# A gated conv-MLP on one core: weights in 2 KB rows, sums of weights by transfers within SBUF, and another order of the products

## The chip, the core and the metric

The kernel is written in the Tile language for Trainium2 and runs on one core. A core has a matrix engine (TensorE, PE in the profile; its weight loads are listed apart as PEld), a vector engine (VectorE, DVE), a scalar engine (ScalarE, ACT), GpSimd (POOL) and SyncE (SP); the last two issue most of the transfers, which 16 DMA engines carry out. SBUF is the memory that the engines read, PSUM the one that PE writes its sums to, in banks. The metric is the device time of one execution in microseconds, the median of several runs.

## What is computed

The program is one inference step of a decoder layer for a prompt of 512 tokens and 8 samples of one token: a mixer, a cross-attention and, as the last third, a gated MLP with a causal convolution between its up-projection and its gate. Only the MLP is touched:

```python
def conv_ffn(xn, prefix, w_up, conv_w, conv_b, w_down):
    T = xn.shape[1]
    up = xn @ w_up
    ext = jnp.concatenate([prefix, up], axis=1)
    c = conv_b
    for k in range(CONV_W):
        c = c + conv_w[k] * ext[:, k:k + T]
    gate, val = jnp.split(c, 2, axis=-1)
    return (jax.nn.silu(gate) * val) @ w_down, ext[:, -(CONV_W - 1):]
```

`w_up` is 1024 x 5632, `w_down` 2816 x 1024, all in fp32. The 520 tokens are held as two halves of 260.

## The kernel before

Every fp32 matrix is split into a high and a low part (`split`: ACT writes `w_hi`, L117, then DVE writes `w_lo`, L120), and a product is three matmuls of 128x128 by 128x260: high by high, high by low, low by high. PE does nothing else in this stage.

*Tiles.* The up-projection is cut into 22 up tiles j of 128 gate and 128 value columns. Tiles 0 to 4 (`up_tile`) and 5, 6 (`up_classic`) are plain products. Tiles 7 to 21 (`up_seven`) take seven products instead of eight by a scheme like Strassen's. With the name of the matrix of mixed inputs of each, the steps of a tile are: s1 (B11), s5 (N1), s2 (B21), s6 (N2), s3 (B22), s7 (T3) and s4 (T4), 12 matmuls each (L1888). They write three banks: a and c are the two halves of one PSUM tile `ps_pp`, b is `ps_t`. s1, s6, s7 and s4 write a; s5 and s3 write c; s2 writes b. Behind s5 ACT copies a and c to `ext`; behind s2 DVE adds b; behind s6 ACT copies a (ext<-ps_pp 128x260); behind s3 DVE adds c (`out12`); behind s7 DVE takes a (`out22`, L1911); behind s4 ACT copies a. The dependence is kept for the PSUM tile, so a product that writes c also comes behind the eviction of a that was written ahead of it.

*Weights.* A product's weights come in units of 256 KB, 128 partitions by 512 values. There are 13 raw units (`w_u`, `raw_x`), used in turn, and a ring of four split ones. s1, s2 and s4 load one block of `w_up` with SP (L1784). s5 and s7 need the sum of two blocks: SP loads the first, then POOL loads the second on top of it with an adding transfer (`both`, L1878). s6's weights are s1's plus s5's raw unit (`sum2`), s3's are s2's plus that (`sum4`); both are adds on DVE ahead of the split (L120, w_u<-w_u and its likes, 128x512). Rows of `w_up` and `w_down` are read from memory in pieces of 128 values, 512 bytes.

*Down-projection.* It is summed over three groups of tiles, 0-6, 7-14, 15-21. The first two groups' 16 column blocks (`down`, two steps each, plain products by `classic`, L1827) stand between the tiles' steps, the rest behind them.

*What sets the order.* The list `steps` is written by hand. A loop goes through it: step m's matmuls are issued together with the split of step m+3 (AHEAD) and with the loads of up to 13 steps ahead (EARLY), as far as raw units are free. A unit is free when the split that reads it is issued; the transfer into it waits for that split and for all that read or write it before. Tile's scheduler may then still move instructions of an engine against each other.

Of the kernel before, what the change touches and what calls it, by code (L numbers as in the profile page):

```python
# [13 lines left out]
OP = mybir.AluOpType  # L14
AX = mybir.AxisListType

P = 128
D = 1024
KT = D // P
# [88 lines left out]
def decoder_step(ctx: ExitStack, tc: tile.TileContext, A, O):  # L108
# [98 lines left out]
    def blocks(hi, lo):  # L207
        return lambda k: (hi[:, k], lo[:, k])
# [1409 lines left out]

    ctx.push(open_psum("ps5", "left", pp=3, t=2))

    w_up = A["w_up"][0]
    w_down = A["w_down"][0]
    PARTS = ((0, 7), (7, 15), (15, FT))
    NA = PARTS[1][0]
    hid = {}
    hid_mid = []
    xs3 = blocks(x3_hi, x3_lo)
    acc4 = ptile(late[0], [P, 2, HT], "acc")
    last_v = last.rearrange("p b (v f) -> p v b f", v=2)

# [8 lines left out]
        ring_at[0] += n  # L1639
        return tuple(t[:, at_ % 2 * 4:at_ % 2 * 4 + 4 * n] for t in ring_w[at_ // 2 % 2])  # L1640

    def up_cols(v, j):
        return slice(v * DFF + j * P, v * DFF + (j + 1) * P)

    def up_products(j):

        raws = [raw_w[j % 2][:, 2 * v:2 * v + 2].rearrange("p u (k c) -> p (u k) c", c=P) for v in range(2)]
        for v in range(2):
            sp.dma_start(raws[v], w_up[:, up_cols(v, j)].rearrange("(k p) c -> p k c", p=P))
        for v in range(2):  # L1650
            w = ring_units(2)
            split(w[0], w[1], raws[v])
            ps = bank("pp")
            project(ps, w, xs3)
            yield ps
# [69 lines left out]
    run(chain(conv(0, 0), conv(0, 1), gate(0)))  # L1725


    NI = KT // 2
    xm4 = [ptile(actp, [P, 4, NI, HT], "act_a", F32R, bufs=2, name="xm4") for _ in range(2)]
    xm3 = ptile(ff, [P, 2, 3, NI, HT], "xm3", F32R)  # L1730
    B11, B21, B22, T3_, N1, N2, T4_ = range(7)
# [36 lines left out]
    taken = set()  # L1768
    behind = []

    def rows(src, k0, n):
        return src[k0 * P:(k0 + n) * P].rearrange("(k p) c -> p k c", p=P)

    def next_unit():
        i = unit_at[0]
        return i % NS if i < 2 * NS else (i - NS) % NU
# [1 line left out]
    def load_unit(src, n=4):  # L1778

        at_ = next_unit()  # L1780
        taken.add(at_)
        unit_at[0] += 1
        u = units[at_].rearrange("p (k c) -> p k c", c=P)[:, :n]
        sp.dma_start(u, src)  # L1784
        return at_, u

    class Step:

        def __init__(self, mm, load=None, prep=None, post=None, held=False):
            self.load_, self.prep_, self.mm_, self.post_, self.held = load, prep, mm, post, held  # L1790

        def load(self):
            if self.load_:
# [8 lines left out]
        def prep(self):  # L1802
            raw = self.prep_() if self.prep_ else self.raw
            if self.load_ and not self.held:
                self.free()
            n = raw.shape[1]
            self.w = tuple(t[:, :n] for t in ring_units(1))
            split(self.w[0], self.w[1], raw)

        def mm(self):  # L1810
            self.mm_(self.w)
# [3 lines left out]
    def classic(ps_of, src, xs, kt, post):  # L1815

        out = []
        for k0 in range(0, kt, 4):
            n = min(4, kt - k0)

            def mm(w, k0=k0, n=n):
                ps = ps_of(k0 == 0)
                for k in range(n):
                    xhi, xlo = xs(k0 + k)
                    for j, (a, x) in enumerate(((w[0], xhi), (w[0], xlo), (w[1], xhi))):
                        for hf in range(2):
                            pe.matmul(ps[:, hf, :HT], a[:, k, :], x[:, hf, :], start=(k0 + k + j == 0),  # L1827
                                      stop=(k0 + k == kt - 1 and j == 2))

            out.append(Step(mm, load=lambda k0=k0, n=n: load_unit(rows(src, k0, n), n), post=post if k0 + n == kt else None))  # L1830
        return out

    def held(tag):
# [9 lines left out]
    def up_classic(j):  # L1843
        out = []
        for v in range(2):
            ps = held("pp")

            def post(v=v, ps=ps):
                evict(j, v, ps())
                behind.append(conv(j, v))  # L1850
                if v:
                    behind.append(gate(j))

            out.append(classic(ps, w_up[:, up_cols(v, j)], xs3, KT, post))
        return out[0] + out[1]

    def down(pi, d, then=None):
        j0, j1 = PARTS[pi]
        ps = held("pp")

        def post():
            tt(hT[:, d], hT[:, d], ps()[:, :, :HT], OP.add)
            if then:
                then()

        return classic(ps, w_down[j0 * P:j1 * P, d * P:(d + 1) * P], lambda k: hid[j0 + k], j1 - j0, post)

    def up_seven(j):

        ac, bb = held("pp"), held("t")  # L1870

        def block(m, s):
            return w_up[:, up_cols(m, j)].rearrange("(i s p) c -> p s i c", s=2, p=P)[:, s]

        def both(a, b):
            def load():
                u = load_unit(a)
                pool.dma_start(u[1], b, accum_op=OP.add)  # L1878
                return u
            return load  # L1880

        def product(ps_of, x, first):
            def mm(w):
                ps = ps_of(first)
                for i in range(NI):
                    xhi, xlo = xm(x, i)
                    for q, (a, b) in enumerate(((w[0], xhi), (w[0], xlo), (w[1], xhi))):
                        pe.matmul(ps, a[:, i, :], b, start=(first and i + q == 0), stop=(i == NI - 1 and q == 2),  # L1888
                                  skip_group_check=True)
            return mm  # L1890

        a_of = lambda new: ac(new)[:, 0, :HT]
        c_of = lambda new: ac()[:, 1, :HT]
        b_of = lambda new: bb(new)[:, :HT]

        def keep():
            e = ext_tile(j)
            acopy(e.rearrange("p v r t -> p (v r) t")[:, 0:4:3, 2:], ac()[:, :, :HT])

        def out11():  # L1900
            o = exts[j][:, 0, 0, 2:]
            tt(o, o, b_of(False), OP.add)

        def out12():
            o = exts[j][:, 0, 1, 2:]
            tt(o, o, c_of(False), OP.add)
            behind.append(conv(j, 0))

        def out22():
            o = exts[j][:, 1, 1, 2:]  # L1910
            dve.scalar_tensor_tensor(o, a_of(False), -1.0, o, op0=OP.mult, op1=OP.subtract)  # L1911

        def out21():
            acopy(exts[j][:, 1, 0, 2:], a_of(False), scale=-1.0)
            behind.extend((conv(j, 1), gate(j)))

        s = {}
        s[1] = Step(product(a_of, B11, True), lambda: load_unit(block(0, 0)), held=True)
        s[5] = Step(product(c_of, N1, True), both(block(1, 0), block(1, 1)), post=keep, held=True)
        s[2] = Step(product(b_of, B21, True), lambda: load_unit(block(0, 1)), post=out11, held=True)  # L1920

        def sum2():
            tt(s[1].raw, s[1].raw, s[5].raw, OP.add)
            s[5].free()
            return s[1].raw

        def sum4():
            tt(s[2].raw, s[2].raw, s[1].raw, OP.add)
            s[1].free()
            s[2].free()  # L1930
            return s[2].raw

        s[6] = Step(product(a_of, N2, False), prep=sum2, post=lambda: acopy(exts[j][:, 0, 1, 2:], a_of(False)))
        s[3] = Step(product(c_of, B22, False), prep=sum4, post=out12)
        s[7] = Step(product(a_of, T3_, False), both(block(0, 0), block(1, 0)), post=out22)
        s[4] = Step(product(a_of, T4_, False), lambda: load_unit(block(1, 1)), post=out21)
        return s
# [1 line left out]
    steps = up_classic(NA - 2) + up_classic(NA - 1)  # L1939
    sevens = [up_seven(j) for j in range(NA, FT)]  # L1940
    downs = [down(0, d) for d in range(KT)] + [down(1, d) for d in range(KT)]
    steps += [sevens[0][i] for i in (1, 5, 2, 6, 3)]
    for n, s in enumerate(sevens):
        t = sevens[n + 1] if n + 1 < len(sevens) else None
        if n:
            steps += downs.pop(0)
        if not t:
            steps += [s[7]] + downs.pop(0) + [s[4]]
        elif n:
            steps += [s[7], t[1], t[5], s[4], t[2], t[6], t[3]]  # L1950
        else:
            steps += [t[1], t[5], s[7], t[2], s[4], t[6], t[3]]
    for x in downs:
        steps += x

# [24 lines left out]
    kt = j1 - j0  # L1980

    def tail_unit(d, k0, n):
        return load_unit(rows(w_down[j0 * P:j1 * P, d * P:(d + 1) * P], k0, n), n)

    AHEAD, EARLY, POPS = 3, 13, 2
    tail_raw = [Step(None, load=lambda d=d, k0=k0: tail_unit(d, k0, min(4, kt - k0))) for d in range(D0, KT) for k0 in (0, 4)]
# [111 lines left out]
def lay_out(x):  # L2098

    def cols(a):  # L2100
# [3 lines left out]
    xs = x["x_sample"][:, 0].reshape(2, 4, KT, P).transpose(3, 2, 0, 1)  # L2104
    pe = x["pe_cmp"][0].reshape(32, P).T
    given = {name: x[name] for name in ("cache_win", "state_pool", "state_ffn", "cache_mem",
                                        "w_pool", "w_out", "w_xq", "w_xkv", "w_xo", "w_up", "w_down")}
    given["x_t"] = np.concatenate([xp, xs], axis=3)
    given["x_row"] = x["x_prompt"][0].reshape(NQB, P, D)
    given["x_row_s"] = x["x_sample"][:, 0]  # L2110
# [3 lines left out]
    given["w_gate_t"] = x["w_in"][0][:, 1792:].reshape(KT, P, 24).transpose(1, 0, 2)  # L2114
    given["w_cmp_t"] = x["w_cmp"][0].reshape(2, 2, 8, P, 64).transpose(3, 0, 2, 1, 4)
    given["w_cmp_e"] = x["w_cmp"][0, 0].reshape(2, 8, P, 64).transpose(3, 1, 0, 2)
    pt = x["page_table"].astype(np.int32)
    given["pages"] = np.concatenate([np.broadcast_to(pt.reshape(1, 64), (P, 64)), np.repeat(pt.reshape(4, 16), 8, axis=1).T], axis=1)
    ck = x["cache_kv"][0].reshape(NPHYS, 8, 16, 4, P)
# [52 lines left out]
```

## Time and profile before

| | us |
|---|---|
| median of 3 runs | 826.23 (826.06 to 830.38) |
| the profiled execution | 827.16 |
| its span, first to last instruction | 825.5 |
| granted clock of PE, mean | 0.996 |
| PE busy, of the span | 808.1 |
| DVE, ACT, POOL busy | 605.5, 448.0, 95.3 |

The page of the profile has, for each engine, its busy time and a line of 40 digits, each the busy tenths of one slice of 20.6 us. The MLP's products fill the last third of the span, from about 448 us. The up tiles with seven products lie between about 530 and 765 us. A row of the timeline has the start, the duration, the engine, the line, the operation with out<-in and, in brackets, the idle time before it with what ended it; "x2" is two instructions in one row. Matmuls are pipelined: one starts every 0.12 us though each is listed with 0.28.

### The profile page before, as it was taken

How to read it: one execution, taken by the hardware profiler on the slowest of the kernel's cores; microseconds unless marked ns; L12 is line 12 of the kernel's file. 1: busy time of each engine (PE TensorE's matmuls, PEld its weight loads, DVE VectorE, ACT ScalarE, POOL GpSimd, SP SyncE). 2: the span in 40 equal slices, each digit the busy share in tenths (PEclk: the TensorE clock that was granted, in tenths of full speed). 3: DMA queues.
4: the chain of work that ended last, by engine and by line, in shares of the span. 5: the costliest groups of instructions: out<-in, count | busy, mean ns of one | idle time of the engine just before them, and what ended most of it. 6: DMA issues, size and time to landing. Idle time of an engine off the chain costs nothing.

```text
span 825.5 us, 17787 instructions
## 1 busy us (share of the span) xinstructions
PE 808.1 (98%) x6889; PEld 754.8 (91%) x6889; DVE 605.5 (73%) x1460; ACT 448.0 (54%) x940; POOL 95.3 (12%) x100
## 2 busy tenths in 40 slices
PE   8999999999999999999999999999999999999996
PEld 8988887987778899999799999999999999999995
DVE  5644586987657766888674799998887887887714
ACT  6742245767665553444343465666666666665541
POOL 1300210000000031000032000111111111100021
PEclk9999999999999999999999999999999999999998
DMA  9988984833222283677443224756766866754422
GB/s 327 251 270 289 413 323 155 290 123 116 77 77 53 60 256 103 204 251 255 137 115 102 75 81 123 156 135 151 166 141 147 169 145 141 158 137 120 160 123 104
DMA packets 146365, 137.87 MB, mean 167 GB/s; under 512 B 6416, under 2 KB 133264, under 8 KB 144088
## 3 DMA queue, kind: packets, MB, share of 16 engines
q1 hardware_dynamic: 127224, 114.63, 44.5%
q0 software_dynamic: 18624, 21.26, 12.3%
q8 instruction: 54, 0.88, 0.4%
q10 hardware_dynamic: 432, 0.84, 0.3%
q14 instruction: 31, 0.25, 0.1%
HBM read 129.56 MB, written 10.69 MB: 170 GB/s over the span
## 4 chain that ended last, share of the span: by engine, by line
PE 85%; DMA 6%; DVE 5%; ACT 2%; issue 1%; SPq 0%; DVEq 0%; POOL 0%; ACTq 0%
PE ps_pp L205 25%; PE ps_pp L1888 16%; PE ps_pp L1827 16%; PE ps_t L1888 3%; PE ps_o L1154 2%; PE ps_pp L2068 2%; PE ps_tb L1071 2%; PE ps_tb L1264 2%; PE ps_sc L1107 2%; DMA WT<-in_w_cmp_e_dram 2%; PE ps_tf L1139 2%; PE ps_x L1465 1%; PE ps_tb L1233 1%; DMA wc_raw<-in_w_cmp_t_dram 1%; PE ps_x L1486 1%
## 5 line engine op out<-in xcount | busy, mean ns | idle before, releaser
L1888 PE MATMUL ps_pp<-xm,w_hi 128*128 128x260 f32 x720 | 133.4, 285 | 0.1
L1888 PEld LDWEIGHTS ps_pp<-xm,w_hi 128*128 128x128 f32 x720 | 110.9, 188 | 2.3 <-ACT ext L117 0.3
L117 ACT ACTIVATE w_hi<-w_u 128x512 fp32r<-128x512 f32 (+2 forms) x110 | 72.7, 662 | 66.5 <-PE ps_pp L1888 22.7
L1888 PE MATMUL ps_pp<-xm,w_lo 128*128 128x260 f32 x360 | 101.5, 282 | 0.0
L120 DVE TENSOR_TENSOR w_lo<-w_u,w_hi 128x512 fp32r<-128x512 f32 (+2 forms) x110 | 80.1, 729 | 16.6 <-ACT w_hi L117 15.3
L1888 PEld LDWEIGHTS ps_pp<-xm,w_lo 128*128 128x128 f32 x360 | 67.7, 188 | 0.0
L120 DVE TENSOR_TENSOR hT<-hT,ps_pp 128x520 f32<-128x520 f32 (+1 forms) x44 | 28.3, 644 | 45.0 <-PE ps_pp L205 17.9
L205 PE MATMUL ps_pp<-x_hi,w_hi 128*128 128x260 f32 x288 | 60.0, 286 | 0.0
L205 PE MATMUL ps_pp<-x_hi,w_lo 128*128 128x260 f32 x288 | 59.6, 285 | 0.0
L205 PE MATMUL ps_pp<-x_lo,w_hi 128*128 128x260 f32 x288 | 58.4, 284 | 0.0
L117 ACT ACTIVATE w_hi<-w_raw 128x1024 fp32r<-128x1024 f32 (+1 forms) x38 | 35.0, 922 | 41.9 <-PE ps_pp L205 31.6
L205 PE MATMUL ps_pp<-xn_hi,w_hi 128*128 128x260 f32 x208 | 45.5, 296 | 1.9 <-ACT w_hi L117 1.9
L205 PEld LDWEIGHTS ps_pp<-x_hi,w_lo 128*128 128x128 f32 x288 | 44.9, 188 | 0.6 <-issue 0.4
L205 PEld LDWEIGHTS ps_pp<-x_hi,w_hi 128*128 128x128 f32 x288 | 44.9, 188 | 0.3
L120 DVE TENSOR_TENSOR w_lo<-w_raw,w_hi 128x1024 fp32r<-128x1024 f32 (+1 forms) x38 | 41.4, 1089 | 5.1 <-ACT w_hi L117 4.8
L1878 POOL DMA_DIRECT2D w_u<-in_w_up_dram x19 | 24.4, 1286 | 178.4 <-DMA w_u<-in_w_up_dram 106.2
L1117 ACT ACTIVATE prob<-prob,mx 128x384 f32<-128x384 f32 (+3 forms) x64 | 35.4, 555 | 17.7 <-DVE mx L1115 17.4
L205 PEld LDWEIGHTS ps_pp<-x_lo,w_hi 128*128 128x128 f32 x288 | 44.5, 188 | 0.4 <-issue 0.4
L205 PE MATMUL ps_pp<-xn_lo,w_hi 128*128 128x260 f32 x208 | 43.6, 289 | 0.1
L205 PE MATMUL ps_pp<-xn_hi,w_lo 128*128 128x260 f32 x208 | 43.5, 289 | 0.0
L120 DVE TENSOR_TENSOR w_lo<-raw_x,w_hi 128x512 fp32r<-128x512 f32 (+1 forms) x53 | 35.8, 675 | 10.3 <-ACT w_hi L117 9.7
L117 ACT ACTIVATE w_hi<-raw_x 128x512 fp32r<-128x512 f32 (+1 forms) x53 | 32.8, 618 | 18.2 <-PE ps_pp L1888 13.2
(495 smaller groups left out, 2309.1 us busy)
## 6 DMA issues: line engine op xcount, KB each, us to landing
w_u<-in_w_up_dram SPq DMA_DIRECT2D x57, 256.0 KB, 3.2
xkr<-in_cache_mem_dram SPq DMA_DIRECT2D x16, 512.0 KB, 4.7
xvr<-in_cache_mem_dram SPq DMA_DIRECT2D x16, 512.0 KB, 7.3
raw_x<-in_w_up_dram SPq DMA_DIRECT2D x26, 256.0 KB, 3.7
Kt<-in_k_t_dram SPq DMA_DIRECT2D x48, 128.0 KB, 2.8
w_u<-in_w_up_dram SPq DMA_DIRECT2D x10, 512.0 KB, 4.3
w_u<-in_w_down_dram SPq DMA_DIRECT2D x20, 256.0 KB, 4.3
w_u<-in_w_up_dram POOLq DMA_DIRECT2D x19, 256.0 KB, 5.9
```

What stands on the lines that cost most here:

```text
L117: act.activation(o, i, AF.Copy, scale=scale)
L120: (eng or dve).tensor_tensor(o, a, b, op=op)
L205: pe.matmul(o, a[:, k, :], x[:, hf, :], start=(k == 0 and j == 0), stop=(k == kt - 1 and j == 2))
L1071: pe.matmul(ps[:, :HT], a[:, k, :], y[x][:, k, hf, :], start=(k + j == 0), stop=(k == 3 and j == 2))
L1107: pe.matmul(ss_[hl][:, 0:n], Qst[:, h, qc], k[:, g, u, 0:n], start=(u == 0), stop=(u == 1), skip_group_check=True)
L1117: act.activation(p[:, 0:nk], p[:, 0:nk], AF.Exp, bias=mx[:, hh:hh + 1], scale=-1.0, accum_out=sm[:, hh:hh + 1])
L1139: pe.transpose(pt[:, hh * P:(hh + 1) * P], pr[hh][:, kb * P:(kb + 1) * P], ident)
L1154: pe.matmul(po[hp * 64:(hp + 1) * 64, g * 256:(g + 1) * 256], Vtok[:, br, kb, g * 64:(g + 1) * 64], pTs[kb][:, hp * 256:(hp + 1) * 256], s ...
L1264: pe.matmul(ps[i], x[:, k, ts_], w[:, kl, :], start=(k == 0 and j == 0), stop=(k == KT - 1 and j == 2))
L1827: pe.matmul(ps[:, hf, :HT], a[:, k, :], x[:, hf, :], start=(k0 + k + j == 0), stop=(k0 + k == kt - 1 and j == 2))
L1878: pool.dma_start(u[1], b, accum_op=OP.add)
L1888: pe.matmul(ps, a[:, i, :], b, start=(first and i + q == 0), stop=(i == NI - 1 and q == 2), skip_group_check=True)
```

## The change

It does three things.

1. The host lays out `w_up` as (2, 22, 128, 2, 4, 128) and `w_down` as (8, 128, 22, 128), so that a unit has one row of 2 KB per partition (4 KB in tiles 0 to 4). In the plain tiles the eight blocks of the sum over 1024 inputs are taken in the order 0, 2, 4, 6, 1, 3, 5, 7 (`xs3`).
2. The two adds of `sum2` and `sum4` are no longer DVE instructions. A step can have a function `after`, called when its split has been issued: s5's adds its raw unit to s1's by a POOL transfer from SBUF to SBUF (L1920), s2's adds s1's to s2's (L1922).
3. The list `steps` has another order: s6 and s7 of a tile stand ahead of the next tile's s1, s3 stands behind that s1, and the down block stands between s2 and s6.

```diff
+    NI = KT // 2
+
+    def xs3(k):
+        kk = 2 * (k % NI) + k // NI
+        return x3_hi[:, kk], x3_lo[:, kk]
...
-            sp.dma_start(raws[v], w_up[:, up_cols(v, j)].rearrange("(k p) c -> p k c", p=P))
+            sp.dma_start(raws[v], w_up[v, j].rearrange("p s i c -> p (s i) c"))
...
             self.w = tuple(t[:, :n] for t in ring_units(1))
             split(self.w[0], self.w[1], raw)
+            if self.after:
+                self.after()
...
-        return classic(ps, w_down[j0 * P:j1 * P, d * P:(d + 1) * P], lambda k: hid[j0 + k], j1 - j0, post)
+        return classic(ps, w_down[d, :, j0:j1], lambda k: hid[j0 + k], j1 - j0, post)
...
         def block(m, s):
-            return w_up[:, up_cols(m, j)].rearrange("(i s p) c -> p s i c", s=2, p=P)[:, s]
+            return w_up[m, j, :, s]
...
-        s[5] = Step(product(c_of, N1, True), both(block(1, 0), block(1, 1)), post=keep, held=True)
-        s[2] = Step(product(b_of, B21, True), lambda: load_unit(block(0, 1)), post=out11, held=True)
+        s[5] = Step(product(c_of, N1, True), both(block(1, 0), block(1, 1)), post=keep, held=True,
+                    after=lambda: pool.dma_start(s[1].raw, s[5].raw, accum_op=OP.add))
+        s[2] = Step(product(b_of, B21, True), lambda: load_unit(block(0, 1)), post=out11, held=True,
+                    after=lambda: pool.dma_start(s[2].raw, s[1].raw, accum_op=OP.add))
 
         def sum2():
-            tt(s[1].raw, s[1].raw, s[5].raw, OP.add)
             s[5].free()
             return s[1].raw
 
         def sum4():
-            tt(s[2].raw, s[2].raw, s[1].raw, OP.add)
             s[1].free()
             s[2].free()
             return s[2].raw
...
-    steps += [sevens[0][i] for i in (1, 5, 2, 6, 3)]
+    steps += [sevens[0][i] for i in (1, 5, 2)]
     for n, s in enumerate(sevens):
         t = sevens[n + 1] if n + 1 < len(sevens) else None
-        if n:
-            steps += downs.pop(0)
         if not t:
-            steps += [s[7]] + downs.pop(0) + [s[4]]
+            steps += downs.pop(0) + [s[3]] + downs.pop(0) + [s[4]]
         elif n:
-            steps += [s[7], t[1], t[5], s[4], t[2], t[6], t[3]]
+            steps += [t[1], s[3], t[5], s[4], t[2]] + downs.pop(0) + [t[6], t[7]]
         else:
-            steps += [t[1], t[5], s[7], t[2], s[4], t[6], t[3]]
+            steps += [t[1], t[5], s[6], s[7], t[2], s[3], s[4], t[6], t[7]]
...
+    given["w_up_t"] = x["w_up"][0].reshape(4, 2, P, 2, FT, P).transpose(3, 4, 2, 1, 0, 5)
+    given["w_down_t"] = x["w_down"][0].reshape(FT, P, KT, P).transpose(2, 1, 0, 3)
```

How this moves PE's instructions in the middle of the stage, for one tile. `ps_pp` with a number is one PSUM tile; xm3 is the input of N1, N2 and T4, xm4 that of B11, B21, B22 and T3; w_hi and w_lo with a number are one unit of the ring. PE before, from the last of N2's matmuls (first row) by the plain down products to the first of B22:

```order
L1888 MATMUL ps_pp_7919<-xm3_6064,w_lo_5887 128x260
L1827 MATMUL ps_pp_8029<-h_hi_6058,w_hi_5884 128x260 x2
L1827 MATMUL ps_pp_8029<-h_lo_6059,w_hi_5884 128x260 x2
L1827 MATMUL ps_pp_8029<-h_hi_6058,w_lo_5885 128x260 x2
L1827 MATMUL ps_pp_8029<-h_hi_6187,w_hi_5884 128x260 x2
L1888 MATMUL ps_pp_7919<-xm4_6062,w_hi_5884 128x260
L1888 MATMUL ps_pp_7919<-xm4_6063,w_hi_5884 128x260
L1888 MATMUL ps_pp_7919<-xm4_6062,w_lo_5885 128x260
```

PE after, from the last of N2's matmuls by the next tile's B11 (ps_pp_8031) to T3's first two:

```order
L1888 MATMUL ps_pp_7848<-xm3_6064,w_lo_5887 128x260
L1888 MATMUL ps_pp_8031<-xm4_6062,w_hi_5884 128x260
L1888 MATMUL ps_pp_8031<-xm4_6063,w_hi_5884 128x260
L1888 MATMUL ps_pp_8031<-xm4_6062,w_lo_5885 128x260
L1888 MATMUL ps_pp_8031<-xm4_6062,w_hi_5884 128x260
L1888 MATMUL ps_pp_8031<-xm4_6063,w_hi_5884 128x260
L1888 MATMUL ps_pp_8031<-xm4_6062,w_lo_5885 128x260
L1888 MATMUL ps_pp_8031<-xm4_6062,w_hi_5884 128x260
L1888 MATMUL ps_pp_8031<-xm4_6063,w_hi_5884 128x260
L1888 MATMUL ps_pp_7848<-xm4_6062,w_hi_5884 128x260
L1888 MATMUL ps_pp_7848<-xm4_6063,w_hi_5884 128x260
```

Eight matmuls stood behind N2 and eight still do; they are now the next tile's own, and what follows them is T3, not B22.

PE before, the last three of T3's matmuls and the next tile's B11, of which 12 and then 12 of N1 follow ahead of T4:

```order
L1888 MATMUL ps_pp_7919<-xm4_6062,w_hi_5886 128x260
L1888 MATMUL ps_pp_7919<-xm4_6063,w_hi_5886 128x260
L1888 MATMUL ps_pp_7919<-xm4_6062,w_lo_5887 128x260
L1888 MATMUL ps_pp_8102<-xm4_6062,w_hi_5884 128x260
L1888 MATMUL ps_pp_8102<-xm4_6063,w_hi_5884 128x260
L1888 MATMUL ps_pp_8102<-xm4_6062,w_lo_5885 128x260
```

PE after, the last three of T3's, then four of the next tile's B11 and one of its N1, and then B22's first:

```order
L1888 MATMUL ps_pp_7848<-xm4_6062,w_hi_5884 128x260
L1888 MATMUL ps_pp_7848<-xm4_6063,w_hi_5884 128x260
L1888 MATMUL ps_pp_7848<-xm4_6062,w_lo_5885 128x260
L1888 MATMUL ps_pp_8031<-xm4_6062,w_lo_5885 128x260
L1888 MATMUL ps_pp_8031<-xm4_6062,w_hi_5884 128x260
L1888 MATMUL ps_pp_8031<-xm4_6063,w_hi_5884 128x260
L1888 MATMUL ps_pp_8031<-xm4_6062,w_lo_5885 128x260
L1888 MATMUL ps_pp_8031<-xm3_6064,w_hi_5886 128x260
L1888 MATMUL ps_pp_7848<-xm4_6062,w_hi_5886 128x260
L1888 MATMUL ps_pp_7848<-xm4_6063,w_hi_5886 128x260
L1888 MATMUL ps_pp_7848<-xm4_6062,w_lo_5887 128x260
```

Behind T3 came 24 matmuls of another PSUM tile ahead of T4; now five come ahead of B22, which writes the other half of T3's tile. The 11 others of N1 follow B22 and stand ahead of T4; before, 34 or 40 plain matmuls and then T3 stood behind B22.

On POOL, the adding loads of `both` (L1878) of five and a half tiles before:

```order
L1878 DMA raw_x_5481<-in_w_up_dram 128x4x128 x2
L1878 DMA w_u_5882<-in_w_up_dram 128x4x128
L1878 DMA w_u_5883<-in_w_up_dram 128x4x128 x2
L1878 DMA raw_x_5481<-in_w_up_dram 128x4x128
L1878 DMA w_u_5882<-in_w_up_dram 128x4x128
L1878 DMA w_u_5883<-in_w_up_dram 128x4x128 x2
L1878 DMA raw_x_5481<-in_w_up_dram 128x4x128 x2
```

and of two tiles after, with the sums within SBUF:

```order
L1920 DMA w_u_5882<-w_u_5882 128x512
L1922 DMA raw_x_5481<-w_u_5882 128x512
L1878 DMA raw_x_5481<-in_w_up_t_dram 128x512
L1878 DMA w_u_5882<-in_w_up_t_dram 128x512
L1920 DMA w_u_5883<-w_u_5883 128x512
L1922 DMA w_u_5883<-w_u_5883 128x512
L1878 DMA w_u_5883<-in_w_up_t_dram 128x512 x2
```

POOL's queue holds, per tile, two sums and then two loads where it held two loads; each load is one row of 512 values per partition instead of four of 128.

More of the change, by code (lines that the diff above doesn't have):

```diff
@@ L1619, in decoder_step @@
     ctx.push(open_psum("ps5", "left", pp=3, t=2))
-    w_up = A["w_up"][0]
-    w_down = A["w_down"][0]
+    w_up = A["w_up_t"]
+    w_down = A["w_down_t"]
     PARTS = ((0, 7), (7, 15), (15, FT))
@@ L1626, in decoder_step @@
     hid_mid = []
-    xs3 = blocks(x3_hi, x3_lo)
+    NI = KT // 2
+    def xs3(k):
+        kk = 2 * (k % NI) + k // NI
+        return x3_hi[:, kk], x3_lo[:, kk]
     acc4 = ptile(late[0], [P, 2, HT], "acc")
@@ L1640, in ring_units @@
         return tuple(t[:, at_ % 2 * 4:at_ % 2 * 4 + 4 * n] for t in ring_w[at_ // 2 % 2])
-    def up_cols(v, j):
-        return slice(v * DFF + j * P, v * DFF + (j + 1) * P)
     def up_products(j):
@@ L1725, in decoder_step @@
     run(chain(conv(0, 0), conv(0, 1), gate(0)))
-    NI = KT // 2
     xm4 = [ptile(actp, [P, 4, NI, HT], "act_a", F32R, bufs=2, name="xm4") for _ in range(2)]
@@ L1769, in decoder_step @@
     behind = []
-    def rows(src, k0, n):
-        return src[k0 * P:(k0 + n) * P].rearrange("(k p) c -> p k c", p=P)
     def next_unit():
@@ L1787, in decoder_step, with __init__ @@
     class Step:
-        def __init__(self, mm, load=None, prep=None, post=None, held=False):
-            self.load_, self.prep_, self.mm_, self.post_, self.held = load, prep, mm, post, held
+        def __init__(self, mm, load=None, prep=None, post=None, held=False, after=None):
+            self.load_, self.prep_, self.mm_, self.post_, self.held, self.after = load, prep, mm, post, held, after
         def load(self):
@@ L1828, in mm @@
                                       stop=(k0 + k == kt - 1 and j == 2))
-            out.append(Step(mm, load=lambda k0=k0, n=n: load_unit(rows(src, k0, n), n), post=post if k0 + n == kt else None))
+            out.append(Step(mm, load=lambda k0=k0, n=n: load_unit(src[:, k0:k0 + n], n), post=post if k0 + n == kt else None))
         return out
@@ L1852, in post @@
                     behind.append(gate(j))
-            out.append(classic(ps, w_up[:, up_cols(v, j)], xs3, KT, post))
+            out.append(classic(ps, w_up[v, j].rearrange("p s i c -> p (s i) c"), xs3, KT, post))
         return out[0] + out[1]
@@ L1982, in tail_unit @@
     def tail_unit(d, k0, n):
-        return load_unit(rows(w_down[j0 * P:j1 * P, d * P:(d + 1) * P], k0, n), n)
+        return load_unit(w_down[d, :, j0 + k0:j0 + k0 + n], n)
     AHEAD, EARLY, POPS = 3, 13, 2
@@ L2106, in lay_out @@
     given = {name: x[name] for name in ("cache_win", "state_pool", "state_ffn", "cache_mem",
-                                        "w_pool", "w_out", "w_xq", "w_xkv", "w_xo", "w_up", "w_down")}
+                                        "w_pool", "w_out", "w_xq", "w_xkv", "w_xo")}
     given["x_t"] = np.concatenate([xp, xs], axis=3)
```

## The prediction

> **What bounds the kernel now.** The page comes first, to see whether one engine fills the span.
>
> ```profile
> span 825.5 us, 17787 instructions
> PE 808.1 (98%) x6889; PEld 754.8 (91%) x6889; DVE 605.5 (73%) x1460; ACT 448.0 (54%) x940; POOL 95.3 (12%) x100
> ...
> PE   8999999999999999999999999999999999999996
> ...
> PEclk9999999999999999999999999999999999999998
> DMA  9988984833222283677443224756766866754422
> ```
>
> TensorE (PE) is busy 98% of the span, at full clock, and the change leaves its matmuls as they are. So the change can win only PE's idle time in the stage that it touches, the last third. The windows of that stage say how much there is, and the list of waits says for what.
>
> ```profile
> core 0: us, PE busy (x) PEld busy (x) DVE busy (x) ACT busy (x) POOL busy (x), PEclk, DMA share, GB/s
> ...
> 500.00:520.00 20.00, 20.00 (x169) 20.00 (x168) 19.90 (x37) 11.39 (x24) 2.60 (x2) 1.00 0.48 119
> ...
> 560.00:580.00 20.00, 20.00 (x167) 19.87 (x166) 16.13 (x30) 13.59 (x30) 4.04 (x4) 1.00 0.70 151
> 580.00:600.00 20.00, 20.00 (x166) 19.74 (x165) 17.08 (x32) 12.54 (x26) 3.68 (x3) 1.00 0.79 166
> ...
> 740.00:760.00 20.00, 20.00 (x167) 19.86 (x167) 16.17 (x29) 11.59 (x23) 0.00 (x0) 1.00 0.36 107
> 760.00:780.00 20.00, 20.00 (x169) 20.00 (x168) 14.54 (x26) 10.94 (x23) 0.79 (x2) 1.00 0.48 160
> ```
> ```profile
> PE ps_t L2046 <- DVE rs_t L2038: 1.3, 1, 1.3
> PE ps_t L2028 <- ACT sqh L2071: 0.5, 1, 0.5
> ```
>
> Between 500 and 826 us PE's only listed waits, 1.8 us, are in the final norm, behind the change. Yet a stretch with seven-product tiles (up_seven) holds 166 or 167 matmuls where one with plain products alone holds 169. At 20.00/169 = 0.118 us each, the missing two or three in 20 us are 0.24 to 0.36 us of pauses too short for the list. The timeline shows one, once per up tile:
>
> ```profile
> 563.98 0.28 PE L1888 MATMUL ps_pp<-xm,w_lo 128*128 128x260 f32 x1
> ...
> 564.10 0.40 PE L1827 MATMUL ps_pp<-h_hi,w_hi 128*128 128x260 f32 x2
> 564.18 0.63 ACT L117 ACTIVATE w_hi<-w_u 128x512 fp32r<-128x512 f32 x1 [0.36 <-PE ps_pp L1888]
> ...
> 564.71 0.37 ACT L117 ACTIVATE ext<-ps_pp 128x260 f32<-128x260 f32 x1
> ...
> 564.82 0.40 PE L1827 MATMUL ps_pp<-h_hi,w_hi 128*128 128x260 f32 x2
> ...
> 565.13 0.30 PEld L1888 LDWEIGHTS ps_pp<-xm,w_hi 128*128 128x128 f32 x2
> 565.14 0.50 PE L1888 MATMUL ps_pp<-xm,w_hi 128*128 128x260 f32 x2
> 565.36 0.19 PEld L1888 LDWEIGHTS ps_pp<-xm,w_lo 128*128 128x128 f32 x1
> 565.48 0.28 PE L1888 MATMUL ps_pp<-xm,w_lo 128*128 128x260 f32 x1
> ```
>
> N2's last matmul starts at 563.98. ScalarE (ACT) first splits weights (0.63), then evicts N2's bank (0.37, done 565.08). PE passes the time with 8 plain matmuls (four rows x2), but B22, which writes the other half of that PSUM tile, loads its weights only at 565.13. Its first matmul was due two slots of 0.12 after 564.82, at 565.06: 0.08 late. The third starts at 565.48 and not 0.24 behind the first: 0.10 more, since the weight load was not ahead. **Price of one handoff with 8 matmuls of cover: 0.18 us.** I count 13 of them, 564.9 to 752.3, one each 15.3 to 16.0 us, and three in the first seven-product tiles (538 to 550) worth 0.75 together. All that the change could remove is 13 x 0.18 + 0.75 = 3.1 us, 0.4%.
>
> **The change part by part.**
>
> *Rows of 2 KB and another k order.* They shorten transfers that PE does not wait for: the list above has no DMA in it. The host's copy lies outside the measured time, and matmuls only swap places inside a sum. Gain 0. What hides it is the lead of loads, 13 units ahead; were that lead gone, a load's landing (3.2 us below) would show, and what longer rows save of it with it.
>
> *Two VectorE (DVE) adds less per tile, two POOL transfers more.*
>
> ```profile
> L120 DVE TENSOR_TENSOR w_u<-w_u 128x512 f32<-128x512 f32 x10 | 6.9, 687 | 0.1
> ...
> L1878 POOL DMA_DIRECT2D w_u<-in_w_up_dram x14 | 18.0, 1286 | 89.0 <-DMA w_u<-in_w_up_dram 86.8 <-issue 2.2
> ```
> ```profile
> L1238 POOL DMA_DIRECT2D out_mem_k_t_dram<-kf x4: 540/540/576, 151.5 to 186.0; - x4
> ...
> DMA to landing us min/median/max: 2.5/4.0/6.7
> ```
> ```profile
> w_u<-in_w_up_dram SPq DMA_DIRECT2D x34, 256.0 KB, 3.2
> ...
> w_u<-in_w_up_dram POOLq DMA_DIRECT2D x14, 256.0 KB, 6.5
> ```
>
> DVE loses 30 x 0.69 = 20.6 us of work over 15 tiles. It was busy 16 to 17 of 20 us, and PE listed no wait for it, so that is worth 0. A sum within SBUF stands nowhere in the trace. Its bounds are POOL's store of 128 rows of 2 KB (0.54 us to issue, 4.0 to land) and POOL's accumulating load in 512-byte rows (1.29 and 6.5). It has the store's shape and adds as the load does; I take the store's 0.54 and, between the two but nearer the store, 4.5. POOL waits for what it issues next: per tile, the first sum must land before the second, the second before the unit is free for SyncE's (SP's) plain load (3.2), that before POOL's accumulating load on top of it, and only behind that in POOL's queue comes the next tile's first sum. The round is 4.5 + 4.5 + 3.2 + 2 x 0.54 = 13.3 us, against the tile's 15.3 to 16.0: hidden, with 2 us to spare. Cost 0; where landing exceeds (16.0 - 3.2 - 1.1)/2 = 5.9 us it is not.
>
> The Trainium skill, page "DMA: Bandwidth & Descriptors", section "Anatomy of one DMA — SWDGE (gpsimd) path", fits such a transfer as 2.0 us plus its bytes over 436 GB/s, an estimate of 2.6 us for 256 KB. The rows (4.0 and 6.5) lie above it; by it the round would only get shorter and the sum would be the same.
>
> *The order on PE.* Three products write where an earlier one is being evicted. *N2 to the next product:* before B22, now T3, 8 matmuls between in both orders, ACT first splitting and then evicting in both: 0.18 as before, difference 0. *B22 after T3:* new. T3 leaves in the a half of the PSUM tile, DVE reads it (L1911), and B22 writes the c half but is ordered behind that read. Only 5 matmuls stand between. DVE's reaction and PE's are in these rows:
>
> ```profile
> 562.53 0.28 PE L1888 MATMUL ps_t<-xm,w_lo 128*128 128x260 f32 x1
> ...
> 562.85 0.43 DVE L120 TENSOR_TENSOR ext<-ext,ps_t 128x260 f32<-128x260 f32 x1
> ```
> ```profile
> 545.31 0.42 DVE L1911 SCALAR_TENSOR_TENSOR ext<-ps_pp,ext 128x260 f32<-128x260 f32 x1
> ...
> 545.52 0.77 PE L1888 MATMUL ps_pp<-xm,w_hi 128*128 128x260 f32 x3
> 545.64 0.68 DVE L120 TENSOR_TENSOR w_lo<-w_u,w_hi 128x512 fp32r<-128x512 f32 x1
> 545.78 0.30 PEld L1888 LDWEIGHTS ps_pp<-xm,w_hi 128*128 128x128 f32 x2 [0.19 <-DVE ext L1911]
> ```
>
> DVE starts 0.32 us after the last matmul's start (562.53 to 562.85), takes 0.42, and the weight load follows 0.05 later (545.73 to 545.78): 0.79 us. Five matmuls and T3's last make 6 x 0.12 = 0.72: 0.07 late, and with the restart's 0.10 it costs 0.17 to 0.18. Twelve tiles (9 to 20): 12 x 0.18 = **+2.2 us**. *T4 after B22:* 11 matmuls between, 12 x 0.12 = 1.44 against 0.79: hidden. This handoff had 34 plain matmuls before, and T3's had a whole 24 of the next tile, which is why the kernel paid for neither.
>
> *Where the new order starts (tiles 7 and 8).* Here the products stand 8, 4, 6, 8, 11 and 6 matmuls behind the eviction that they wait for. By the same sum, 0.79 against (cover + 1) x 0.12, a cover of 4 costs 0.19 + 0.10 = 0.3 and one of 6 only part of the restart, 0.1. A cover of 8 behind one ACT split costs 0.18; the second of the 8s has two splits on ACT ahead of its eviction, 0.63 more less the cover's slack: about 0.6. The last 6 is an eviction that finds DVE in a 0.69 split half the time: 0.4. Together 0.18 + 0.3 + 0.1 + 0.6 + 0.4 = 1.6 against 0.75 before: **+0.85 us**. Bounds: 0 (each covered) and +2.
>
> **Sum.** The profiled execution took 827.16 us, of which 1.66 lie outside the span, and 0.93 more than the median of the three runs. 827.16 + 2.2 + 0.85 = 830.2; on the median's scale 826.23 + 3.0 = **829.2 us**.
>
> **Rivals.**
>
> 1. *Nothing shows:* the handoff behind T3 is quicker than 0.72 and the start costs as before. The margin is 0.07 us, against a 0.06 scatter of DVE's start (0.32 here, 0.38 where it waits for two things), so this can be. The edits are then all hidden: 826.2 to 827.
>
> 2. *All handoffs hidden, faster:* PE would have other work at each, and the 3.1 us of pauses go: 826.23 - 3.1 = 823.1. Interleaving two tiles puts one tile's products where the other's bank is being read, which speaks for it; against it, T3 and B22 still write their own tile 8 and 5 matmuls behind an eviction. That independent groups should rotate through PSUM banks, so that one's evacuation overlaps the next one's matmuls, is what the Trainium skill says on the page "Perfetto Trace Analysis", section "Optimizing Tensor Performance"; the pause at 565.1 agrees that a reused tile makes PE wait.
>
> 3. *DVE or ACT has another instruction in hand when T3 ends:* the eviction starts up to a split (0.69) late. With half of that in each of 12 tiles, 12 x 0.35 = 4.2 more: 833.4. DVE's order has two splits just ahead of L1911, released long before, and DVE has 1.4 us less work per tile, which speaks against it.
>
> 4. *The sums become the bound, slower:* if they land like today's accumulating loads, 6.5 us, the round on POOL's queue is 6.5 + 6.5 + 3.2 + 1.1 = 17.3, 1.3 us longer than the tile. Over 13 tiles 17 us, less some 3 us of lead in the units: about 840. It decides at 5.9 us of landing. For it: the DMA engines are already 0.6 to 0.8 busy in these windows, and a sum moves 256 KB out and back. Against it: a quarter of the rows to describe, and loads in longer rows leave the engines emptier.
>
> The same Trainium skill page on DMA, section "Issuing engines are not separate DMA queues", says that all issuers' transfers run on the same 16 engines and interleave. That speaks for the fourth rival; the share of 0.70 in 560 to 580 us is what this case shows of it.
>
> **How the numbers follow.** Forecast 0.62, nothing shows 0.10, all hidden 0.04, late evictions 0.12, sums as the bound 0.12. A measurement tells about 0.5% from no change: below 822.1 or above 830.4. The all-hidden case reaches the first only if a little more goes, so faster gets 0.03. Slower takes rivals 3 and 4 and that part of the forecast, 0.12, in which the start or the handoffs cost 1.2 us more: 0.36; the rest, 0.61, is same. The range leaves out most of the all-hidden case and the sums as the bound: 824.5 to 836.5.
>
> **What would show it.** Right: in each tile two short pauses, T3 behind ACT's eviction of N2 and B22 behind L1911, of about 0.18 us each; windows of 20 us with 164 to 166 matmuls; no wait of PE for a DMA or a split; sums landing below 5.9 us. Wrong: POOL's wait for its own sums followed by PE waiting for a split of w_u or raw_x (rival 4), L1911 starting over 0.5 us behind T3's last matmul (rival 3), 168 or 169 matmuls in the windows (rival 2).

## The result and the profile after

The change made the kernel slower: 838.81 us median of 5 runs against 827.25 of before, ratio 1.0148 (95% interval 1.0121 to 1.0176). The forecast was 829.2, with a range up to 836.5. The profiled execution has a span of 837.2 us, 11.7 more than before.

The page and the windows of the changed kernel (columns as in the prediction): PE has as much work, but in some stretches of 20 us it does 149 to 154 matmuls where it did 167 or 168, and is idle for 1.4 to 2.0 us.

```profile
span 837.2 us, 17817 instructions
...
PE 811.0 (97%) x6889; PEld 754.9 (90%) x6889; DVE 588.7 (70%) x1430; ACT 442.3 (53%) x940; POOL 109.2 (13%) x130
```
```profile
580.00:600.00 20.00, 20.00 (x163) 19.46 (x162) 14.45 (x26) 11.39 (x24) 4.13 (x6) 1.00 0.72 157
600.00:620.00 20.00, 18.56 (x154) 18.22 (x153) 14.31 (x27) 11.51 (x25) 4.59 (x6) 1.00 0.74 159
620.00:640.00 20.00, 17.99 (x149) 17.65 (x148) 13.48 (x25) 10.57 (x25) 4.34 (x5) 1.00 0.71 157
...
680.00:700.00 20.00, 18.46 (x149) 18.05 (x149) 13.16 (x24) 10.01 (x22) 3.71 (x5) 1.00 0.75 184
```

PE's list of waits, which had only the final norm before, now begins with one that names ACT's eviction to `ext`:

```profile
PE ps_pp L1888 <- ACT ext L117: 9.5, 8, 2.0
```

One of these eight waits in the timeline, the rows of ACT, DVE, SP and PE:

```profile
628.75 0.40 PE L1888 MATMUL ps_pp<-xm,w_hi 128*128 128x260 f32 x2
629.65 0.33 SPq L1782 DMA_DIRECT2D raw_x<-in_w_up_t_dram  x1
629.68 1.15 ACT L117 ACTIVATE w_hi<-w_u 128x512 fp32r<-128x512 f32 x2 [2.03 <-DMA w_u<-raw_x]
...
630.34 1.29 DVE L120 TENSOR_TENSOR w_lo<-w_u,w_hi 128x512 fp32r<-128x512 f32 x2 [1.35 <-ACT w_hi L117]
630.73 0.37 ACT L117 ACTIVATE ext<-ps_pp 128x260 f32<-128x260 f32 x1
...
631.15 0.51 PE L1888 MATMUL ps_pp<-xm,w_hi 128*128 128x260 f32 x2 [2.01 <-ACT ext L117]
```

PE has done N2 and the next tile's eight matmuls, and T3 waits for N2's eviction. The eviction is a copy of 0.37 us whose input has long been there. It stands in ACT's queue behind two splits, and the first of them waits 2.03 us for the second sum in SBUF (w_u<-raw_x) to land. The list names the eviction, and the late one is the transfer. Why it is late shows POOL's timeline, of two neighbouring tiles (L1920 and L1922 are the sums, L1878 the adding loads):

```profile
617.03 0.93 POOL L1920 DMA_DIRECT2D raw_x<-raw_x  x1
622.30 0.86 POOL L1922 DMA_DIRECT2D w_u<-raw_x  x1 [4.34 <-DMA raw_x<-raw_x]
626.49 0.86 POOL L1878 DMA_DIRECT2D w_u<-in_w_up_t_dram  x1 [3.32 <-DMA w_u<-in_w_up_t_dram]
633.07 0.86 POOL L1878 DMA_DIRECT2D raw_x<-in_w_up_t_dram  x1 [5.71 <-DMA raw_x<-in_w_up_t_dram]
633.60 1.22 POOL L1920 DMA_DIRECT2D w_u<-w_u  x1
```

The first sum is issued at 617.03, the second when that has landed, at 622.30. It lands at 629.65; only then does SP load into the unit that it has read (the row at 629.65 above); the load lands at 633.07, POOL issues the adding load on top of it, and behind that the next tile's first sum at 633.60. The round takes 16.57 us, where a tile needs 15.3 to 16.0 us of PE. From first sum to first sum, the ten rounds between 564 and 734 us take 16.1 to 18.3 us, 17.0 on average. What the first sum needs was there long before: it waits for nothing of its own when its turn comes, and only its place in the queue holds it.

How long the sums take from issue to landing (minimum, median, maximum), from the views of their two lines, L1920 for the first and L1922 for the second:

```profile
DMA to landing us min/median/max: 4.4/4.9/5.7
```
```profile
DMA to landing us min/median/max: 3.6/6.4/7.5
```

The second is the slower one, and SP's timeline shows what is moved beside it. SP had waited 7.9 us for the first sum, too (raw_x<-raw_x), with other loads behind that wait in its queue, and lets four go at the same moment, around the 622.30 of the second sum:

```profile
621.82 0.33 SPq L1782 DMA_DIRECT2D raw_x<-in_w_up_t_dram  x1
622.24 0.86 SPq L1782 DMA_DIRECT2D w_u<-in_w_up_t_dram  x2
623.19 0.38 SPq L1782 DMA_DIRECT2D w_u<-in_w_down_t_dram  x1
```

The handoff that the forecast was built on is there as well, in the timeline of the changed kernel. T3's last matmul is the first of the row at 615.01 (the second is already B11's). DVE reads the bank at 615.32. The row x3 at 615.60 holds N1's matmul and B22's first two; B22 starts 0.09 late and loses 0.10 more behind its first matmul, so that the row lasts 0.72 in place of 0.53:

```profile
615.01 0.40 PE L1888 MATMUL ps_pp<-xm,w_lo 128*128 128x260 f32 x2
...
615.32 0.43 DVE L1911 SCALAR_TENSOR_TENSOR ext<-ps_pp,ext 128x260 f32<-128x260 f32 x1 [1.26 <-PE ps_pp L1888]
...
615.60 0.72 PE L1888 MATMUL ps_pp<-xm,w_hi 128*128 128x260 f32 x3
```

Summed over all starts of matmuls between 528 and 780 us, the pauses (what a start is over 0.12 us behind the last, from 0.05 on) are 3.2 us before and 15.9 after: 12.7 more, against 11.7 more of span. The nine longest pauses ahead of T3, in one of the first tiles and eight later, hold 11.0 of them.

### The profile page after: what moved, and what is told of

The parts are those of the page before. It is cut to its first block, busy times and chain, and to the rows that moved or that the text cites. A ratio compares the mean times of both kernels' runs of the same rounds, so it can differ in the third digit from the quotient of the medians.

```text
span 837.2 us, 17817 instructions
## 1 busy us (share of the span) xinstructions
PE 811.0 (97%) x6889; PEld 754.9 (90%) x6889; DVE 588.7 (70%) x1430; ACT 442.3 (53%) x940; POOL 109.2 (13%) x130
## 5 line engine op out<-in xcount | busy, mean ns | idle before, releaser
L1888 PE MATMUL ps_pp<-xm,w_hi 128*128 128x260 f32 x720 | 135.3, 287 | 9.6 <-ACT ext L117 9.5
L1888 PE MATMUL ps_pp<-xm,w_lo 128*128 128x260 f32 x360 | 99.1, 283 | 0.0
L1827 PE MATMUL ps_pp<-h_mid,w_hi 128*128 128x260 f32 x256 | 41.3, 283 | 0.0
```

## The experiments

Each ratio is to the kernel before, run beside it on the same chip. The times are medians; the ratios are worked out from the single runs and differ a little from the quotients of the medians.

**Sums back on DVE.** The new order and the rows stay. The two functions `after` go and `tt(s[1].raw, s[1].raw, s[5].raw, OP.add)` and `tt(s[2].raw, s[2].raw, s[1].raw, OP.add)` come back into `sum2` and `sum4`.

> The changed kernel with both sums of weights back on DVE; rows of 2 KB and the new order stay. Theory A (the two adding transfers in SBUF, 4.8 and 6.6 us to land, make a round on POOL's queue of over 16 us, and ACT's split that waits for the second stands ahead of N2's eviction): the long pauses ahead of T3 go, the two short ones of 0.19 us per tile stay, about 3 us over before: 829.5 to 831 where before is 827. Theory B (the new order itself leaves T3 too little cover, whoever adds): the pauses of 0.4 to 2.2 us stay, 836 to 839.

828.75 us against 826.26, ratio 1.0033 (1.0010 to 1.0056). PE's list names only the final norm again. The pauses add up to 5.9 us, 2.7 more than before: the two short ones of each tile and the start. So the order costs about what the forecast said (2.5 to 2.7 us for 3.0), and the other four fifths of the loss (1.48% against 0.33%) are with the transfers. Theory B is out.

**Only the rows.** The kernel before with `w_up_t`, `w_down_t` and `xs3`.

> The kernel before with nothing but the rows of 2 KB and the other k order. Theory A: no wait of PE goes or comes, within 1 us of before (826 to 828). Theory C (longer packets hold the DMA engines longer, 84 ns where 27 were, and make other transfers late): 830 or more. Were rows of 512 bytes a hidden cost: under 824.

825.91 against 826.26, ratio 0.9983 (0.9965 to 1.0000): 0.35 us between the medians, so within 1 us, but 1.4 us by the ratio, whose interval ends at no change. Theory C is out. A small gain of the rows is not.

**The old order with the sums as transfers.** The list `steps` of before in the changed kernel:

```diff
-            steps += [t[1], s[3], t[5], s[4], t[2]] + downs.pop(0) + [t[6], t[7]]
+            steps += [s[7], t[1], t[5], s[4], t[2], t[6], t[3]]
```

> The changed kernel with the order of steps of before; the sums stay transfers. Theory A: between the split of N1's weights and that of B22's lie four steps of 12 matmuls, 5.8 us, where the two sums need 4.8 + 6.6 = 11.4 us; at least 5 us per tile are missing in 15 tiles, 880 to 930. Theory B: the old cover is back, so the long pauses go, 827 to 830.

855.61 against 826.26, ratio 1.0335 (1.0295 to 1.0375). Slower in the way that theory A says, but by 29 us where it asked for 53 or more: pauses of 0.9 to 1.0 us ahead of B22 in most tiles and of up to 1.8 ahead of the down products in seven, besides two longer ones at the start. The number of 53 rested on landings that this kernel doesn't have: here the sums land in 3.3 and 4.2 us in the median, not in 4.8 and 6.6. Four steps on PE may also have been too short a measure of the time that they have, since the splits run three steps ahead; how much each has to do with the miss was not followed. With the sums as transfers, the new order loses 12 us where the old one loses 29, so it does help them; but neither order makes them pay.

**One sum each.** The first sum stays a transfer, the second is on DVE (`tt` in `sum4`).

> The changed kernel with the second sum (for B22) on DVE and the first one left a transfer. Theory A: the round on POOL's queue is 4.8 for the sum, 3.4 for the plain load and some 2 for issues, far below the tile's 16, so 829.5 to 832. Theory B: 836 to 839, the order is the same. Theory D (any transfer in SBUF on POOL's queue is late for its split, not the chain of two): long pauses stay, now ahead of N2, over 834.

836.31 against 826.26, ratio 1.0102 (1.0053 to 1.0151). A miss for theory A as it stood then, which counted only the transfers of the round. PE now waits for DVE's eviction of B22, 5.4 us in all, and DVE's rows at one of these waits show why:

```profile
652.51 0.69 DVE L120 TENSOR_TENSOR w_u<-w_u,raw_x 128x512 f32<-128x512 f32 x1 [1.71 <-DMA raw_x<-w_u]
653.12 0.42 DVE L120 TENSOR_TENSOR ext<-ext,ps_pp 128x260 f32<-128x260 f32 x1
...
653.68 0.36 PE L1888 MATMUL ps_pp<-xm,w_hi 128*128 128x260 f32 x1 [1.28 <-DVE ext L120]
```

DVE's add waits for the first sum, and the eviction stands behind it. It is the same picture with another engine. POOL's rows showed the first sum issued at 645.88, 0.83 us behind an adding load that had waited 5.14 us for its plain load. That gave theory A': the sum is late because of its place behind that load.

**The first sum ahead of the adding load.** The adding load of T3's weights is kept back until the tile's first sum has been issued; both sums stay transfers:

```diff
+        def add2():
+            pool.dma_start(s[1].raw, s[5].raw, accum_op=OP.add)
+            first.append(next(i for i in reversed(nc.cur_bb.bb.instructions) if i.engine == EN.Pool))
+            for add in held_add:
+                with tc.issue_after(first[0]):
+                    add()
```

> The changed kernel with one thing moved in POOL's queue: a tile's first sum in SBUF no longer stands behind the adding load of T3's weights of the same tile, but ahead of it. Both sums stay transfers. Theory A' (the round is sum, sum, plain load and the first sum of the next tile behind the adding load that waits for it; 4.8 + 6.6 + 3.4 + 1.7 = 16.5 us): what is left of the round is second sum, plain load and issues, about 11.5 us, so the long pauses go, 829 to 832, with sums that land as late as before. Theory D (a sum's landing is too long for the split that reads it, wherever it stands): 835 or more.

830.86 against 828.20, ratio 1.0029 (1.0008 to 1.0049). One pause over 0.3 us is left, in the first tiles, as PE's list of waits shows it (the products' line is L1904 in this kernel):

```profile
PE ps_pp L1904 <- ACT ext L117: 2.5, 1, 2.5
```

And the same sums of 256 KB land sooner. Issue to landing in this kernel, minimum, median and maximum, of the line of the first sum and of the second:

```profile
DMA to landing us min/median/max: 3.3/3.3/3.9
```
```profile
DMA to landing us min/median/max: 3.5/3.6/8.0
```

POOL's rows of one tile and a half (L1892 is the first sum here, L1938 the second) show the new place, and that the sums now wait for a split on DVE, so for PE's pace, and no longer for a transfer:

```profile
618.26 0.86 POOL L1938 DMA_DIRECT2D w_u<-raw_x  x1 [5.03 <-DVE w_lo L120]
620.59 0.86 POOL L1878 DMA_DIRECT2D w_u<-in_w_up_t_dram  x1 [1.47 <-DMA w_u<-in_w_up_t_dram]
627.01 0.86 POOL L1892 DMA_DIRECT2D w_u<-w_u  x1 [5.55 <-DVE w_lo L120]
627.54 1.21 POOL L1878 DMA_DIRECT2D raw_x<-in_w_up_t_dram  x1
```

With nothing but a place in a queue changed, four fifths of the loss are gone, as with the sums on DVE. The 4.9 and 6.4 us were then not the price of a sum, but of a sum beside what was let go with it: in the changed kernel four of SP's loads start from 0.5 us ahead of the second sum to 0.9 behind it, here three from 0.9 ahead to 2.7 behind. No run moved SP's loads alone. Theory A' had the sums landing as late as before, which they do not, so this run changes the place and the landings together. That long landings in any place were the trouble, theory D, is out: the time is 830.9 and not 835.

**A quarter of each sum.** `[:, 0:1]` on both operands of both sums; the rest of the adds is left out.

> The changed kernel with a quarter of each sum transferred, 512 bytes of each 2 KB row; three quarters of the adds are left out. Theory A': each sum lands sooner by what its bytes cost, I guess 3.5 to 4.5 us instead of 4.8 and 6.6, the round falls to 13 to 14 us, below the tile: 829 to 832. Theory E (not how long the sums take but that splits and loads have to wait for a transfer of POOL at all): 836 to 839.

830.15 against 828.20, ratio 1.0037 (1.0009 to 1.0065), no pause over 0.3 us. Issue to landing in this kernel, first and second sum:

```profile
DMA to landing us min/median/max: 2.7/4.9/5.6
```
```profile
DMA to landing us min/median/max: 2.3/2.8/5.5
```

The dependences are all still there, and the links of the round add up to 4.9 + 2.8 + 3.5 for the plain load + 1.5 = 12.7 us: below the tile. So it is the length of the round that counts, and theory E is out. The first sum lands in 4.9 us, as in the change, and stands behind the adding load, as in the change; that alone makes no pause. That it lands no sooner with a quarter of the bytes I had not expected. It is issued 0.5 us behind an adding load of 256 KB.

**The eviction ahead of the late split.** In the changed kernel the split of B22's weights is issued on ACT behind N2's eviction. For that, the loop also issues every step's matmuls ahead of the split of the step three further on, not behind it:

```diff
+            i = gone.get(self.behind)
+            with tc.issue_after(i) if i is not None else nullcontext():
+                split(self.w[0], self.w[1], raw)
```

> The changed kernel with ACT's split of B22's weights put behind its eviction of N2; sums and POOL's queue as in the change. Theory A': T3 no longer waits for the late split, but the round of 16.5 us is still longer than the tile's 15.3 to 16, so a part of the pause comes back as B22 or N2 waiting for its weights: 831 to 836. Theory F (it is only ACT's queue, the split that waits ahead of the eviction): 829 to 830.5, no pause over 0.3 us left.

838.19 against 828.20, ratio 1.0123 (1.0073 to 1.0174). T3 waits no more, and the pause has moved to the weights, by PE's list of waits (L1894 is the products' line here):

```profile
PE ps_pp L1894 <- DVE w_lo L120: 3.5, 4, 1.7
...
PE ps_pp L1894 <- ACT w_hi L117: 1.1, 2, 0.6
```

Theory F is out: ACT's queue decided where the pause showed, not that there was one. The time lies 2 us above what theory A' gave. Before, at 828.20, is itself 1 to 2 us above that of the earlier runs (827.25 and 826.26), which is half of it or more. The other edit in the loop may have a part, too; this was not followed.

**One sum, and ahead.** The kernel with the second sum on DVE and the first moved as in `add2`.

> The kernel with the second sum on DVE (836.3 in its run, where no gain over the change's 838.8 could be told) with the first sum moved ahead of the adding load of T3's weights in POOL's queue. Theory A': there, too, the sum came late because it stood behind that load, and DVE, whose add waits for it, held back B22's eviction; so 829 to 831 where before is 826 to 828, and no pause over 0.3 us between 560 and 760. Theory G (a sum by a transfer costs DVE's queue that much wherever it stands): 834 or more.

827.94 against 825.94, ratio 1.0040 (1.0022 to 1.0058), no pause over 0.3 us, and DVE's list of waits names no sum any more. The time lies 1 us under the range that was given; theory G is out. This settles the miss above: there, too, it was the place in the queue.

**The other way: more cover.** Sums on DVE, rows of 2 KB, and the order of before with the down block's two steps apart:

```diff
-            steps += [s[7], t[1], t[5], s[4], t[2], t[6], t[3]]
+            steps += [s[7], t[1], t[5], s[4], t[2], t[6], d[0], t[3], d[1]]
```

> No part of the change but its rows: sums on DVE, the order of before, with one edit. The first step of each down block (24 matmuls) stands between N2 and B22 and the second (18 or 24) between B22 and T3, so every eviction has at least 18 matmuls beside it. By the price of a handoff, 0.18 us with 8 matmuls of cover and nothing with 12 or more, 13 x 0.18 = 2.4 us go: 823 to 824.5 where before is 826.3. Rival: the pauses come back at another place (DVE is busier there): 826 to 827.

824.27 against 828.20, ratio 0.9962 (0.9940 to 0.9984). The time lies in the range, but by luck: before is 828.20 here and not 826.3, so 3.9 us went where 2.4 were worked out. The rival is out. To see what the rows have to do with it, the same order was run in rows of 512 bytes.

> The kernel before, in its own rows of 512 bytes and with sums on DVE, with only the down block's two steps put behind N2 and behind B22. By the price of a handoff as before 13 x 0.18 us less, and a little of the start: 823 to 824.5 where before is 826.3, the same as with rows of 2 KB. Rival (the rows carry a part of that gain): 825 or more.

825.02 against 825.94, ratio 1.0001 (0.9978 to 1.0024): no difference to be told, and by the number the rival's 825 or more. Its profile has the same pauses gone (0.4 us left of 3.2), but its times spread from 821.9 to 832.5, the high ones at a lower granted clock (0.985 to 0.989).

> The same kernel as the one with rows of 2 KB, sums on DVE and the down block's steps put apart (824.3 against 828.2 of before in its run), with more rounds, since the one in rows of 512 bytes showed the same pauses gone in its profile but no gain that its spread lets one tell. By the price of a handoff: 0.995 to 0.998 of before. If the gain of the first run was chance: 0.999 to 1.001.

822.88 against 826.82, ratio 0.9946 (0.9920 to 0.9971). This version is faster than both kernels. Windows of it, as in the part on what bounds the kernel:

```profile
560.00:580.00 20.00, 20.00 (x169) 20.00 (x168) 16.95 (x32) 12.02 (x25) 2.58 (x3) 1.00 0.66 169
580.00:600.00 20.00, 20.00 (x169) 20.00 (x169) 17.40 (x33) 12.79 (x27) 1.72 (x2) 1.00 0.51 138
```

169 matmuls, as in the stretches of plain products; 0.4 us of pauses are left. The pauses account for 2.8 of the 3.9 us between the medians. Whether the rows have a part in the rest stays open: by themselves they gained 0.35 us by the medians and 1.4 by the ratio, with an interval from 2.9 to nothing, and in rows of 512 bytes the order's gain did not stand out of the spread.

## Why the prediction was wrong

*What bounds the kernel:* right. PE has no work to lose here, and the change could only add pauses or take them away. The pauses that could be taken were 3.1 us by the forecast; the order that takes them gained 3.9 us in each of its two runs in rows of 2 KB, and none that could be told in rows of 512 bytes.

*Rows of 2 KB, gain 0:* not refuted. The gain is 0.35 us by the medians and 1.4 by the ratio, and the interval only just reaches no change.

*The adds taken from DVE, worth 0:* not contradicted. With them back on DVE, PE's list still names no wait for DVE but the one in the final norm.

*The new order, +3.0 us:* right in mechanism, and nearly in size. With the sums on DVE it is 2.5 us between the medians, 2.7 in pauses. B22 came 0.09 us late and lost 0.10 to 0.11 more on its restart, in tiles 9 to 20, where 0.07 and 0.10 were worked out; that is 2.4 us for the forecast's 2.2. T4, with 11 matmuls of cover, paid nothing, as forecast. The start, in tiles 7 and 8, was over-sized: its pauses there are 0.96 us where they were 0.75, so 0.2 more and not 0.85. The two misses partly cancel in the sum.

*The sums: hidden, "4.5 + 4.5 + 3.2 + 2 x 0.54 = 13.3 us, against the tile's 15.3 to 16.0".* This is the step that failed. The round was the right one, link by link, and the fourth rival, about 840 us with 0.12, is what happened. The term that was mis-sized is the landing of a sum, and above all that of the second: 4.5 us were taken, and it took 7.3 in the tile shown and 6.4 in the median. The first took 4.7 and 4.9. With 3.4 for the plain load in place of 3.2, and the two issues of about 0.5 as forecast, the tile's round is 16.6 us in place of 13.3. I had taken the landing "nearer the store", and with another place in the queue a sum does land in 3.3 to 3.6 us, less than I took. What was missed is that the links of a round are not independent. The landing of the first sum lets four of SP's plain loads go together with the second sum, and the adding load lets the first sum go 0.5 us behind itself. So for the second sum the bound of 6.5, from a load among other loads, was the nearer one. That SP's loads are what makes it late is read from the traces and not shown by a run of its own.

The Trainium skill, page "DMA: Bandwidth & Descriptors", section "Issuing engines are not separate DMA queues", was quoted for that rival: transfers of all issuers interleave on the same 16 engines. These runs agree, with 3.6 us in the median for the second sum where SP's loads are spread out and 6.4 where it starts with four of them. The estimate of 2.6 us for 256 KB, by the fit in the Trainium skill's section "Anatomy of one DMA — SWDGE (gpsimd) path" on the same page, lies below all of these.

*What was to be seen of it:* named as POOL's wait and then "PE waiting for a split". PE's list named an eviction instead, since ACT had the late split ahead of it. PE waited for the split itself when the eviction was moved ahead.

*Rival 3, evictions late by a split in hand:* an eviction was late on ACT in eight tiles, but because the split ahead of it waited for a transfer; with the sums on DVE it went back to 0.2 us.

## What to carry to other kernels

A transfer that replaces an add of 0.69 us on an engine with time to spare has to be priced as a link of the round that it joins: follow its queue to the next transfer of the same kind, add all landings and issues, and take landings as they are when a link lets other transfers go at the same moment, not as they are at a quiet one. In an in-order queue the order can matter as much as the duration: here one sum moved ahead of a load that it did not need was worth as much as taking both sums away, or as moving a quarter of their bytes. And where PE is full, count the matmuls between an eviction and the next write to its bank: 8 behind a split and an eviction on ACT, and 5 behind an eviction on DVE, cost 0.2 us each time here; 11 (T4 in the new order) and more cost nothing.

## What the runs showed of the hardware

An adding transfer of 256 KB within SBUF takes POOL 0.86 us to issue where nothing was issued just before, and mostly 1.2 us where an adding load went 0.5 us ahead; in the kernel with the first sum ahead it lands in 3.3 us in the median as the first sum and in 3.6 as the second, with SP's loads 0.9 us or more away, and in 5.1 to 7.5 us with four of SP's loads around its issue (the second sum of the changed kernel, from 570 us on). With a quarter of its bytes the second sum lands in 2.8 us in the median instead of 6.4; but in most tiles SP's loads no longer go with it there, and against the 3.6 of the kernel with the first sum ahead it is 0.8 sooner. Where two of SP's loads go in the 0.7 us ahead of it, in four tiles, even the quarter takes 3.9 to 4.4 us. The first sum, right behind an adding load of 256 KB, lands no sooner with a quarter (4.9); what it would take without that load and with a quarter of the bytes was not tried.
